# Seven block products for eight on the last two k-tiles of layer B's pairs, in a two-layer attention trunk

## The chip, the core and the metric

The kernel runs on one core of a Trainium2 chip. The metric is the time on the device in microseconds (us). Engines run side by side, each through its own list of instructions in order, and wait for each other by semaphores: TensorE (PE in the profile, its weight loads PEld), VectorE (DVE), ScalarE (ACT), GpSimd (POOL) and SyncE (SP), which issues DMA transfers. POOL issues transfers too.

## What is computed

256 positions of width 2048 go through one layer of chunked attention (A) and one of forgetting attention (B), 32 heads of 128 each, everything in float32. Cut to what matters here:

```python
# layer A
h = rms_norm(x, a_norm);  q, k, v, g = split(h @ a_w_in, 4)      # 2048 -> 4 x 4096
o = chunked_relbias_attention(q, k, v)
x = x + (o * silu(g)) @ a_w_out                                   # 4096 -> 2048
# layer B
h_kv = rms_norm(x, kv_norm);  k, v = split(h_kv @ kv_w, 2)
h = rms_norm(x, b_norm);      q, g = split(h @ b_w_in, 2)
sc = q @ k.T / sqrt(128) + decay                                  # causal, decay from a cumulative sum
o = softmax(sc) @ v
x = x + (o * silu(g)) @ b_w_out
out = rms_norm(x, final_norm)
```

## The kernel before

**Projections.** Each projection is cut into units of 512 output columns. A unit accumulates in two PSUM tiles, one for each half of 128 positions (`acc[0]`, `acc[1]`). It reads its weights in sub-blocks of two k-tiles (256 rows), 512 KB each; with 2048 rows that is eight sub-blocks a unit. To keep float32 precision, each weight block is split into a high and a low part: ACT writes `hi` (a rounded copy), DVE writes `lo` (the rest), and x is split likewise. A block product is then three matmuls of 512 columns (`hi` by x's high part, `lo` by x's high part, `hi` by x's low part). A sub-block is 2 k-tiles x 2 halves x 3 = 12 matmuls.

**Pairs.** Two heads form a group; there are 16 groups. In each layer a group needs two units: `aqk` and `avg` in layer A, `bqg` (q and gate) and `bkv` (k and v) in layer B. These two units are a pair. In layer B the weights are also multiplied by a norm's gain, a number for each row: ACT applies it in `hi` (L243), DVE in `lo` (L244), one k-tile (half a sub-block, 512 columns) at a time. In layer A there is no gain, and one instruction does a whole sub-block (L248, L249).

**Seven products.** The last sub-block of both units of a pair forms a 2 x 2 by 2 x 2 block product (two halves of positions, two k-tiles, two units). Eight block products can be had with seven, for some sums of x's blocks (`sum_up`, once for all groups) and of weight blocks. Layer A's pairs 1 to 15 do that (class `Quad`): `split` makes differences of the two raw blocks on DVE and four splits of them (`quad_hi`, `quad_lo` 0 to 3), of which three are 1024 wide and one 512; `step` issues 21 matmuls, of which four products go to PSUM tiles of their own (p1, p5, p7, p6) and three straight into the units' accumulators; ACT copies p1 out, four adds on DVE make four combinations in `comb`, and each accumulator has one of them added when it is read. Layer B's pairs take all eight sub-blocks of both units plainly.

**The feed.** `Feed` runs ahead of TensorE: six raw buffers are loaded by SP, four `hi` and four `lo` buffers hold splits. A split can be written when the matmuls of the fourth split before it are done. What stands in which order on each engine is set by the scheduler of the framework, from the order of the code and its own estimates; `tc.issue_after` pins some places.

**Attention beside it.** While a pair's matmuls run, the attention of the group before goes through the other engines, cut into steps by `yield`; `drive` calls them at the sub-blocks given by `B1_STEPS` (first unit), `B2_STEPS` (second) and `OLD_B_STEPS`. For layer B: ACT evacuates k from the accumulator of `bkv` into `qk` (L510), DVE transposes 32 x 32 blocks of q and k (`first<-qk`, L501), POOL issues 16 transfers that put the blocks in place (`sums<-first`, L504; the tile is called `sums`, since the attention uses half of that buffer), and ACT and DVE split them (`wide`, `q`). TensorE makes the scores (`s1p`, `s0p`), DVE adds the bias and finds maxima, ACT takes exponentials. DVE transposes the probabilities and the gates (`sgY`), POOL transfers them (`sgZ`), they are split (`wide<-sgZ`), TensorE makes `op`, and DVE multiplies by the gate (`oT`). On TensorE the `op` of the group before stands behind a pair's second sub-block of `bqg`, the scores of this one behind its seventh.

Of the kernel before, what the change touches and what calls it, by code (L numbers as in the profile page):

```python
# [76 lines left out]
def trunk(ctx, tc, x, x_t, gains, a_w_in, a_rel, a_w_out, kv_w, f_w, f_b, b_w_in, b_w_out, final_norm, out):  # L77
# [111 lines left out]
    class Feed:  # L189
# [31 lines left out]
        def prepare(self, ahead=True, parts=(slice(None),)):  # L221
# [12 lines left out]
            if 0 <= h < spec["kept"]:  # L234
                both = big_tile([P, 2, IL, KB, HN], F32R, f"{nm}_keep{b}")
                hi, lo = both[:, 0], both[:, 1]
            else:
                hi = stream.tile([P, IL, KB, HN], F32R, name=f"{nm}_hi{b}", tag="hi", bufs=SPLIT)
                lo = stream.tile([P, IL, KB, HN], F32R, name=f"{nm}_lo{b}", tag="lo", bufs=SPLIT)
            if spec["g0"] is not None:  # L240
                for j in range(KB):
# [1 line left out]
                    act.activation(hi[:, :, j], raw[:, :, j], AF.Copy, scale=gk)  # L243
                    dve.scalar_tensor_tensor(lo[:, :, j], raw[:, :, j], gk, r32(hi[:, :, j]),  # L244
                                             op0=OP.mult, op1=OP.subtract)
# [32 lines left out]
    class Quad:  # L278

        def __init__(self, all_, specs, b, first, last):  # L280
            self.all, self.specs, self.b, self.first, self.last = all_, specs, b, first, last

        def split(self, i):
# [3 lines left out]
            if not i:  # L287
                if not self.all.w:
                    feed.behind(t[:, :, 0, :1], -1)
                with tc.issue_after(feed.by_dve.ins) if self.all.w else nullcontext():  # L290
                    dve.tensor_sub(t[:, :, 0], two[:, :, 0], one[:, :, 0])
                    dve.tensor_sub(t[:, :, 1], two[:, :, 1], two[:, :, 0])
            src = [one, t, two[:, :, 1:], one][i]
            n = src.shape[2]
            hi = stream.tile([P, IL, KB, HN], F32R, name=f"quad_hi{i}", tag="hi", bufs=SPLIT)
            lo = stream.tile([P, IL, KB, HN], F32R, name=f"quad_lo{i}", tag="lo", bufs=SPLIT)
            feed.by_act = act.activation(hi[:, :, :n], src, AF.Copy)
            feed.by_dve = dve.tensor_sub(lo[:, :, :n], src, r32(hi[:, :, :n]))
            if not i:
                dve.tensor_sub(one[:, :, 0], two[:, :, 1], t[:, :, 0])  # L300
                dve.tensor_sub(one[:, :, 1], one[:, :, 1], one[:, :, 0])
# [738 lines left out]
```

## Time and profile before

| | us |
|---|---|
| median of three runs (1738.96 to 1740.59) | 1739.95 |
| the profiled execution | 1738.73 |
| its span | 1737.0 |
| PE busy | 1723.2 (99%) |
| DVE busy | 1377.9 (79%) |
| ACT busy | 1139.4 (66%) |
| POOL busy | 517.0 (30%) |

The profile is of one execution. A group's mean duration is from the start of an instruction to its end; since an engine begins the next one before the last has ended, the distance between two starts is shorter. In the chain of work that ended last, a row is a stretch of one engine: its start, its length, and the instructions in it. In the timeline a row has start, length, engine, line, operation, `out<-in`, shapes and count, and in brackets the idle time before it with what ended it.

### The profile page before, as it was taken

How to read it: one execution, taken by the hardware profiler on the slowest of the kernel's cores; microseconds unless marked ns; L12 is line 12 of the kernel's file. 1: busy time of each engine (PE TensorE's matmuls, PEld its weight loads, DVE VectorE, ACT ScalarE, POOL GpSimd, SP SyncE). 2: the span in 40 equal slices, each digit the busy share in tenths (PEclk: the TensorE clock that was granted, in tenths of full speed). 3: DMA queues.
4: the chain of work that ended last, by engine and by line, in shares of the span. 5: the costliest groups of instructions: out<-in, count | busy, mean ns of one | idle time of the engine just before them, and what ended most of it. 6: DMA issues, size and time to landing. Idle time of an engine off the chain costs nothing.

```text
span 1737.0 us, 25888 instructions
## 1 busy us (share of the span) xinstructions
PE 1723.2 (99%) x8303; PEld 1513.8 (87%) x8303; DVE 1377.9 (79%) x2066; ACT 1139.4 (66%) x2151; POOL 517.0 (30%) x1071
## 2 busy tenths in 40 slices
PE   9999999999999999999999999999999999999997
PEld 7888888888888888888888888888888888888886
DVE  7888888888888888989876777777777777776887
ACT  6666666666666666655567777777777777675554
POOL 1332333333333333112204333333333333333000
PEclk9999999999999999999999999999999999999999
DMA  8766767667767677677757767676777776777654
GB/s 301 245 227 227 232 230 229 232 225 230 233 226 227 227 227 227 205 252 256 241 203 235 228 226 225 226 227 226 227 227 226 227 228 227 248 229 231 224 194 145
DMA packets 143656, 396.37 MB, mean 228 GB/s; under 512 B 31104, under 2 KB 38560, under 8 KB 143392
## 3 DMA queue, kind: packets, MB, share of 16 engines
q1 hardware_dynamic: 107472, 354.25, 62.3%
q0 software_dynamic: 32256, 37.29, 6.6%
q10 hardware_dynamic: 3792, 3.17, 0.6%
q8 instruction: 66, 1.08, 0.3%
q14 instruction: 70, 0.57, 0.1%
HBM read 351.05 MB, written 4.23 MB: 205 GB/s over the span
## 4 chain that ended last, share of the span: by engine, by line
PE 97%; DVE 1%; DMA 1%; ACT 1%; SPq 0%; issue 0%; DVEq 0%; ACTq 0%
PE bkv_acc L185 19%; PE bqg_acc L185 19%; PE avg_acc L185 17%; PE aqk_acc L185 16%; PE bo_acc L185 8%; PE ao_acc L185 7%; PE p L532 1%; PE p L531 1%; PE p L530 1%; PE s0p L554 1%; PE op L594 1%; PE op L532 0%; PE s1p L532 0%; PE s1p L531 0%; PE op L531 0%; PE op L530 0%
## 5 line engine op out<-in xcount | busy, mean ns | idle before, releaser
L504 POOL DMA_DIRECT2D sums<-first x448 | 219.9, 498 | 324.8 <-DVE wide L523 147.7
L504 POOL DMA_DIRECT2D sgZ<-sgY x512 | 250.7, 497 | 173.8 <-DVE sgY L501 90.1
L244 DVE SCALAR_TENSOR_TENSOR bqg_lo<-bqg_raw,gain,bqg_hi 128x512 fp32r<-128x512 f32 x256 | 183.0, 752 | 88.1 <-ACT bqg_hi L243 88.1
L243 ACT ACTIVATE bqg_hi<-bqg_raw,gain 128x512 fp32r<-128x512 f32 x256 | 170.8, 713 | 110.0 <-PE bqg_acc L185 51.9
L244 DVE SCALAR_TENSOR_TENSOR bkv_lo<-bkv_raw,gain,bkv_hi 128x512 fp32r<-128x512 f32 x256 | 180.3, 749 | 40.8 <-ACT bkv_hi L243 39.2
L185 PE MATMUL bqg_acc<-bqg_hi,x1Th 128*128 128x512 f32 x512 | 191.4, 384 | 0.0
L185 PE MATMUL bkv_acc<-bkv_hi,x1Th 128*128 128x512 f32 x512 | 189.0, 379 | 0.0
L185 PE MATMUL bkv_acc<-bkv_hi,x1Tl 128*128 128x512 f32 x512 | 188.8, 379 | 0.0
L185 PE MATMUL bkv_acc<-bkv_lo,x1Th 128*128 128x512 f32 x512 | 188.8, 379 | 0.0
L185 PE MATMUL bqg_acc<-bqg_hi,x1Tl 128*128 128x512 f32 x512 | 188.8, 379 | 0.0
L185 PE MATMUL bqg_acc<-bqg_lo,x1Th 128*128 128x512 f32 x512 | 188.8, 379 | 0.0
L243 ACT ACTIVATE bkv_hi<-bkv_raw,gain 128x512 fp32r<-128x512 f32 x256 | 167.8, 713 | 25.8 <-PE bqg_acc L185 19.9
L185 PE MATMUL aqk_acc<-aqk_hi,xTh 128*128 128x512 f32 x452 | 167.6, 382 | 1.7 <-ACT aqk_hi L248 1.7
L185 PE MATMUL avg_acc<-avg_hi,xTh 128*128 128x512 f32 x452 | 167.4, 382 | 0.0
L185 PE MATMUL aqk_acc<-aqk_lo,xTh 128*128 128x512 f32 x452 | 166.3, 379 | 1.0 <-DVE aqk_lo L249 1.0
L185 PE MATMUL avg_acc<-avg_lo,xTh 128*128 128x512 f32 x452 | 166.1, 379 | 0.0
L185 PE MATMUL avg_acc<-avg_hi,xTl 128*128 128x512 f32 x452 | 166.1, 379 | 0.0
L185 PE MATMUL aqk_acc<-aqk_hi,xTl 128*128 128x512 f32 x452 | 166.1, 379 | 0.0
L248 ACT ACTIVATE avg_hi<-avg_raw 128x1024 fp32r<-128x1024 f32 x112 | 116.1, 1050 | 76.1 <-PE avg_acc L185 50.5
L249 DVE TENSOR_TENSOR avg_lo<-avg_raw,avg_hi 128x1024 fp32r<-128x1024 f32 x112 | 136.8, 1222 | 31.0 <-ACT avg_hi L248 31.0
L249 DVE TENSOR_TENSOR aqk_lo<-aqk_raw,aqk_hi 128x1024 fp32r<-128x1024 f32 x110 | 134.1, 1223 | 24.8 <-ACT aqk_hi L248 17.0
L248 ACT ACTIVATE aqk_hi<-aqk_raw 128x1024 fp32r<-128x1024 f32 x110 | 115.6, 1051 | 42.2 <-PE avg_acc L185 31.6
(345 smaller groups left out, 3926.2 us busy)
## 6 DMA issues: line engine op xcount, KB each, us to landing
bqg_raw<-in_b_w_in SPq DMA_DIRECT2D x128, 512.0 KB, 4.3
bkv_raw<-in_kv_w SPq DMA_DIRECT2D x128, 512.0 KB, 4.1
avg_raw<-in_a_w_in SPq DMA_DIRECT2D x127, 512.0 KB, 4.6
aqk_raw<-in_a_w_in SPq DMA_DIRECT2D x125, 512.0 KB, 4.5
ao_raw<-in_a_w_out SPq DMA_DIRECT2D x64, 512.0 KB, 4.5
bo_raw<-in_b_w_out SPq DMA_DIRECT2D x64, 512.0 KB, 4.2
sgZ<-sgY POOLq DMA_DIRECT2D x512, 40.0 KB, 3.9
sums<-first POOLq DMA_DIRECT2D x448, 32.0 KB, 3.7
```

The lines of the kernel that those rows point to most:

```text
L185: pe.matmul(acc[t], x[:, t * P:(t + 1) * P], w, start=t not in begun, stop=last and i == 2)
L243: act.activation(hi[:, :, j], raw[:, :, j], AF.Copy, scale=gk)
L244: dve.scalar_tensor_tensor(lo[:, :, j], raw[:, :, j], gk, r32(hi[:, :, j]), op0=OP.mult, op1=OP.subtract)
L248: self.by_act = act.activation(hi[:, :, j], raw[:, :, j], AF.Copy)
L249: self.by_dve = dve.tensor_sub(lo[:, :, j], raw[:, :, j], r32(hi[:, :, j]))
L504: queues[j].dma_start(out=r32(z)[j * SQ:(j + 1) * SQ, i], in_=y[i * SQ:(i + 1) * SQ, j])
L530: pe.matmul(out_, a[0], b[0], start=start, stop=False)
L531: pe.matmul(out_, a[0], b[1], start=False, stop=False)
L532: pe.matmul(out_, a[1], b[0], start=False, stop=stop)
L554: pe.matmul(s0p[:, i], q0[:, i], qkT[:, HG + i, 0], start=True, stop=True)
L594: pe.matmul(op[:, i, 1::NT], v1[:, i * DH:(i + 1) * DH], pT[:, i, NT], start=False, stop=i == HG - 1)
```

## The change

Layer B's pairs 1 to 15 get the seven products too. The last sub-blocks of `bqg` and `bkv` are left out of the plain lists; a `Quad` of both stands behind the third sub-block of `bkv` (`QUAD_STEP_B = 3`, after the seven plain ones of `bqg`). Since the weights of layer B carry gains, `split` first scales the two raw blocks in place on ACT, a k-tile at a time, four instructions in all. `comb` then holds the combinations; `add_whole` adds them onto the accumulators: `qg`'s right behind the products, where `open_b` reads them, and `kv`'s when that unit is done. The sums of x for the last two k-tiles of layer B are made once, in group 0. And the layout of all weight blocks changes: a sub-block was `[2 halves, 2 k-tiles, 256]` a partition, with a k-tile's two halves (columns that alternate in the matmul's reading) 2 KB apart, and is now `[2 k-tiles, 2 halves, 256]`, with the halves 1 KB apart and a k-tile in one run of 2 KB. The host packs the weights in that order.

```diff
+QUAD_STEP_B = 3
 def cols(v, j):
-    return v[:, :, j].rearrange("p a n -> p n a")
+    return v[:, j].rearrange("p a n -> p n a")
 ...
         def buffer(self, name):
-            ... stream.tile([P, IL, KB, HN], F32, name=name, tag="raw", bufs=RAW)
+            ... stream.tile([P, KB, IL, HN], F32, name=name, tag="raw", bufs=RAW)
 ...
     class Quad:
         def __init__(self, all_, specs, b, first, last):
+            self.w = specs[0]["g0"] is not None or all_.w
 ...
         def split(self, i):
             if not i:
-                if not self.all.w:
-                    feed.behind(t[:, :, 0, :1], -1)
+                if not self.w:
+                    feed.behind(t[:, 0, :, :1], -1)
+                if self.specs[0]["g0"] is not None:
+                    with tc.issue_after(feed.by_act.ins):
+                        for raw, sp_ in zip(self.raw, self.specs):
+                            for j in range(KB):
+                                gk = gain[:, sp_["g0"] + self.b * KB + j:][:, :1]
+                                act.activation(raw[:, j], raw[:, j], AF.Copy, scale=gk)
-                with tc.issue_after(feed.by_dve.ins) if self.all.w else nullcontext():
+                with tc.issue_after(feed.by_dve.ins) if self.w else nullcontext():
 ...
+    def paired(specs, n):
+        quad = Quad(a_quads, specs, KD // KB - 1, True, True)
+        plain = whole(specs[0]) + whole(specs[1])
+        todo.extend(plain[:n] + [(None, quad)] + plain[n:])
+        return quad
+    a_pairs = [paired(qkvg[2 * g:2 * g + 2], QUAD_STEP) for g in range(1, NG)]
 ...
-        qkvg.append(spec(f"bqg{g}", b_w_in[g], KD, g0=GB))
-        qkvg.append(spec(f"bkv{g}", kv_w[g], KD, g0=GKV))
+        qkvg.append(spec(f"bqg{g}", b_w_in[g], KD, g0=GB, quads=g > 0))
+        qkvg.append(spec(f"bkv{g}", kv_w[g], KD, g0=GKV, quads=g > 0))
 ...
+    b_pairs = [paired(qkvg[2 * g:2 * g + 2], KD // KB - 1 + QUAD_STEP_B) for g in range(NG + 1, 2 * NG)]
 ...
+    def add_whole(acc, i):
+        out = [a_quads.comb[:, i * NT + t] for t in range(NT)]
+        for t in range(NT):
+            dve.tensor_add(out[t], acc[t], out[t])
+        return out
 ...
-    def open_b(accs):
-        qk, qg = rows(UN, "qk"), accs["qg"]
+    def open_b(accs, g):
+        qk, qg = rows(UN, "qk"), add_whole(accs["qg"], 0) if g else accs["qg"]
 ...
-        accs["qg"] = drive(unit(x1T), prev if g else last[0], B1_STEPS if g else {2: 99}, {}, old, OLD_B_STEPS)
-        accs["kv"] = drive(unit(x1T), prev if g else fg, B2_STEPS if g else FORGET_STEPS, {2: lambda: open_b(accs)})
+        if g:
+            first, second = (Unit(x1T, next(order)) for _ in range(2))
+            accs["qg"] = drive(rest(first), prev, B1_STEPS, {}, old, OLD_B_STEPS)
+            def products():
+                b_pairs[g - 1].step(x1T, first, second)
+                open_b(accs, g)
+            kv = drive(rest(second), prev, B2_STEPS, {QUAD_STEP_B - 1: products})
+            accs["kv"] = add_whole(kv, 1)
+        else:
+            accs["qg"] = drive(unit(x1T), last[0], {2: 99})
+            accs["kv"] = drive(unit(x1T), fg, FORGET_STEPS, {2: lambda: open_b(accs, g)})
+            a_quads.sum_up(x1T, KD // KB - 1, sums[:, 0], a_quads.comb)
 ...
-        out.append(cols.reshape(k // KB, KB, P, HN, IL).transpose(0, 2, 4, 1, 3))
+        out.append(cols.reshape(k // KB, KB, P, HN, IL).transpose(0, 2, 1, 4, 3))
```

How this moves instructions, at three places of group 7 (the other groups are alike). In the names, the number behind `hi`, `lo` and `raw` is the sub-block, and the last number is the buffer's.

ScalarE behind the landing of the transposed q and k in `sums`, first before (L522 and L546 split q and k, L243 the sub-blocks of kv, L570 takes exponentials), then after:

```order
L522 ACTIVATE wide_11922<-sums_104 128x2x128
L522 ACTIVATE q1_11924<-sums_104 128x128
L522 ACTIVATE wide_11922<-sums_104 128x2x128
L522 ACTIVATE q1_11924<-sums_104 128x128
L546 ACTIVATE q0_11934<-sums_104 128x256
L243 ACTIVATE bkv7_hi0_11902<-bkv7_raw0_11728,gain_83 128x2x256 x2
L243 ACTIVATE bkv7_hi1_11937<-bkv7_raw1_11782,gain_83 128x2x256 x2
L243 ACTIVATE bkv7_hi2_11979<-bkv7_raw2_11808,gain_83 128x2x256 x2
L570 ACTIVATE sg_11967,sm_11969<-sg_11967,nm_11968 128x256 x2
```

```order
L535 ACTIVATE wide_12063<-sums_104 128x2x128
L535 ACTIVATE q1_12065<-sums_104 128x128
L535 ACTIVATE wide_12063<-sums_104 128x2x128
L244 ACTIVATE bkv7_hi1_12043<-bkv7_raw1_11865,gain_83 128x512 x2
L535 ACTIVATE q1_12065<-sums_104 128x128
L559 ACTIVATE q0_12075<-sums_104 128x256
L244 ACTIVATE bkv7_hi2_12078<-bkv7_raw2_11923,gain_83 128x512 x2
L297 ACTIVATE bqg7_raw7_11949<-bqg7_raw7_11949,gain_83 128x512 x2
L297 ACTIVATE bkv7_raw7_11951<-bkv7_raw7_11951,gain_83 128x512 x2
L305 ACTIVATE quad_hi0_12126<-bqg7_raw7_11949 128x1024
```

kv's first sub-block has moved ahead of the landing, and four scalings of the raw blocks and the first product's `hi` stand behind its third.

VectorE from the third sub-block of kv on (`sg<-s1p` adds the bias to the scores, L568 or L581 finds the maxima, `csc` is the softmax's factor), first before, then after:

```order
L244 SCALAR_TENSOR_TENSOR bkv7_lo2_11980<-bkv7_raw2_11808,gain_83,bkv7_hi2_11979 128x2x256
L564 SCALAR_TENSOR_TENSOR sg_11967<-s1p_11957,cb_11742 128x256 x2
L567 SCALAR_TENSOR_TENSOR sg_11967<-s0p_11958,d0_11763 128x2x128
L568 TENSOR_REDUCE nm_11968<-sg_11967 128x2 x2
L244 SCALAR_TENSOR_TENSOR bkv7_lo2_11980<-bkv7_raw2_11808,gain_83,bkv7_hi2_11979 128x2x256
L576 RECIPROCAL csc_12041<-sm_11969 128x4
L577 TENSOR_TENSOR csc_12041<-csc_12041,half_b_8598 128x4
L244 SCALAR_TENSOR_TENSOR bkv7_lo3_12002<-bkv7_raw3_11842,gain_83,bkv7_hi3_12001 128x2x256 x2
L244 SCALAR_TENSOR_TENSOR bkv7_lo4_12022<-bkv7_raw4_11862,gain_83,bkv7_hi4_12021 128x2x256 x2
L501 STREAM_TRANSPOSE sgY_12048<-sg_11967 128x1280
```

```order
L299 TENSOR_TENSOR first1_102<-bkv7_raw7_11951,bqg7_raw7_11949 128x512
L577 SCALAR_TENSOR_TENSOR sg_12108<-s1p_12098,cb_11881 128x256 x2
L580 SCALAR_TENSOR_TENSOR sg_12108<-s0p_12099,d0_11902 128x2x128
L581 TENSOR_REDUCE nm_12109<-sg_12108 128x2 x2
L300 TENSOR_TENSOR first1_102<-bkv7_raw7_11951 128x512
L306 TENSOR_TENSOR quad_lo0_12127<-bqg7_raw7_11949,quad_hi0_12126 128x1024
L589 RECIPROCAL csc_12160<-sm_12110 128x4
L308 TENSOR_TENSOR bqg7_raw7_11949<-bkv7_raw7_11951,first1_102 128x512
L590 TENSOR_TENSOR csc_12160<-csc_12160,half_b_8598 128x4
L309 TENSOR_TENSOR bqg7_raw7_11949<-bqg7_raw7_11949 128x512
L306 TENSOR_TENSOR quad_lo1_12145<-first1_102,quad_hi1_12144 128x1024
L514 STREAM_TRANSPOSE sgY_12167<-sg_12108 128x1280
```

The first difference of raw blocks, which needs three of ACT's scalings, now stands ahead of the scores, and the products' differences and splits between the scores and the gate transpose.

VectorE from the end of kv to the transpose of q and k (`first<-qk`), first before, then after; L735 is `add_whole`:

```order
L244 SCALAR_TENSOR_TENSOR bkv7_lo7_12116<-bkv7_raw7_11943,gain_83,bkv7_hi7_12115 128x2x256 x2
L244 SCALAR_TENSOR_TENSOR bqg8_lo0_12136<-bqg8_raw0_11985,gain_83,bqg8_hi0_12135 128x2x256 x2
L244 SCALAR_TENSOR_TENSOR bqg8_lo1_12156<-bqg8_raw1_12007,gain_83,bqg8_hi1_12155 128x2x256 x2
L244 SCALAR_TENSOR_TENSOR bqg8_lo2_12176<-bqg8_raw2_12027,gain_83,bqg8_hi2_12175 128x2x256 x2
L501 STREAM_TRANSPOSE first1_102<-qk_12087 128x1024
```

```order
L352 TENSOR_TENSOR comb_103<-comb_103,p5_12205 128x512
L245 SCALAR_TENSOR_TENSOR bkv7_lo6_12275<-bkv7_raw6_12084,gain_83,bkv7_hi6_12274 128x512
L735 TENSOR_TENSOR comb_103<-bqg7_acc1_11914,comb_103 128x512
L639 SCALAR_TENSOR_TENSOR gs_12269<-gs_12269,comb_103 128x256
L245 SCALAR_TENSOR_TENSOR bqg8_lo0_12295<-bqg8_raw0_12190,gain_83,bqg8_hi0_12294 128x512 x2
L639 SCALAR_TENSOR_TENSOR gs_12269<-gs_12269,comb_103 128x256
L245 SCALAR_TENSOR_TENSOR bqg8_lo1_12315<-bqg8_raw1_12212,gain_83,bqg8_hi1_12314 128x512 x2
L245 SCALAR_TENSOR_TENSOR bqg8_lo2_12335<-bqg8_raw2_12226,gain_83,bqg8_hi2_12334 128x512 x2
L735 TENSOR_TENSOR comb_103<-bkv7_acc0_11915,comb_103 128x512
L735 TENSOR_TENSOR comb_103<-bkv7_acc1_11916,comb_103 128x512
L245 SCALAR_TENSOR_TENSOR bqg8_lo3_12393<-bqg8_raw3_12240,gain_83,bqg8_hi3_12392 128x512 x2
L514 STREAM_TRANSPOSE first1_102<-qk_12264 128x1024
```

The combinations, the gate's products and two adds onto kv have come in front of the transpose, with one sub-block more of the next unit.

More of the change, by code (lines that the diff above doesn't have):

```diff
@@ L198, in buffer @@
         def buffer(self, name):
-            return self.early.pop(0) if self.early else stream.tile([P, IL, KB, HN], F32, name=name, tag="raw",
+            return self.early.pop(0) if self.early else stream.tile([P, KB, IL, HN], F32, name=name, tag="raw",
                                                                     bufs=RAW)
@@ L206, in load @@
                     first(j)
-                sp.dma_start(out=raw[:, :, j], in_=spec["w"][b][:, :, j])
+                sp.dma_start(out=raw[:, j], in_=spec["w"][b][:, j])
             return raw
@@ L263, in behind @@
         def behind(self, dst, n):
-            act.activation(dst, r32(self.ready[n][0][:, :, 0, :1]), AF.Copy)
+            act.activation(dst, r32(self.ready[n][0][:, 0, :, :1]), AF.Copy)
         def fill(self):
@@ L287, in split @@
             if not i:
-                if not self.all.w:
-                    feed.behind(t[:, :, 0, :1], -1)
-                with tc.issue_after(feed.by_dve.ins) if self.all.w else nullcontext():
[L291 to L298, printed above, removed]
+                if not self.w:
[7 more added lines that the diff above has]
+                with tc.issue_after(feed.by_dve.ins) if self.w else nullcontext():
+                    dve.tensor_sub(t[:, 0], two[:, 0], one[:, 0])
+                    dve.tensor_sub(t[:, 1], two[:, 1], two[:, 0])
+            src = [one, t, two[:, 1:], one][i]
+            n = src.shape[1]
+            hi = stream.tile([P, KB, IL, HN], F32R, name=f"quad_hi{i}", tag="hi", bufs=SPLIT)
+            lo = stream.tile([P, KB, IL, HN], F32R, name=f"quad_lo{i}", tag="lo", bufs=SPLIT)
+            feed.by_act = act.activation(hi[:, :n], src, AF.Copy)
+            feed.by_dve = dve.tensor_sub(lo[:, :n], src, r32(hi[:, :n]))
             if not i:
-                dve.tensor_sub(one[:, :, 0], two[:, :, 1], t[:, :, 0])
-                dve.tensor_sub(one[:, :, 1], one[:, :, 1], one[:, :, 0])
+                dve.tensor_sub(one[:, 0], two[:, 1], t[:, 0])
+                dve.tensor_sub(one[:, 1], one[:, 1], one[:, 0])
             return hi, lo
@@ L627, in gate_from @@
         return gs
-    first = [big_tile([P, 2, IL, KB, HN], F32, name=f"first{i}") for i in range(2)]
+    first = [big_tile([P, 2, KB, IL, HN], F32, name=f"first{i}") for i in range(2)]
     feed.early += [first[i][:, j] for i in range(2) for j in range(2)]
```

30 lines of the change are left out of this document (11 added, 19 removed).

## The prediction

> **What bounds the kernel now.** I read the head of the page, then the chain that ended last in order of time, then each engine's busy time by stage, and then the timeline of VectorE (DVE), ScalarE (ACT) and GpSimd (POOL) around one pair of layer B.
>
> ```profile
> span 1737.0 us, 25888 instructions
> PE 1723.2 (99%) x8303; PEld 1513.8 (87%) x8303; DVE 1377.9 (79%) x2066; ACT 1139.4 (66%) x2151; POOL 517.0 (30%) x1071
> ...
> 352.39 2.59 PE aqk_acc L185 x12
> 395.42 2.59 PE aqk_acc L185 x12
> 1037.14 5.18 PE bqg_acc L185 x24
> 1057.51 2.59 PE bqg_acc L185 x12
> 1060.10 20.72 PE bkv_acc L185 x96
> 1080.82 5.18 PE bqg_acc L185 x24
> 1561.22 5.18 PE bo_acc L185 x24
> ```
>
> TensorE is the bound. Twelve matmuls take 2.59 us, 215.9 ns each. A pair of layer B lasts 1080.82 - 1037.14 = 43.68 us; a pair of layer A, which already has seven products, 395.42 - 352.39 = 43.03. The difference, 0.65, is three matmuls (3 x 0.2159 = 0.648): no pair stalls in either layer. The profiled execution took 1738.73 us, 1.73 over its span; the median of the three runs shown is 1739.95, 1.2 above it. I make the sum against 1738.73 and add the 1.2 at the end.
>
> ```profile
> 355.30:398.30 43.00, 43.00 (x212) 37.93 (x211) 36.95 (x52) 27.98 (x51) 13.89 (x29) 1.00 0.70 229
> 1043.40:1087.10 43.70, 43.70 (x214) 38.55 (x213) 31.65 (x54) 31.33 (x69) 16.05 (x34) 1.00 0.71 226
> ```
>
> By stretch (length, then PE, PEld, DVE, ACT, POOL busy): DVE works 36.95 us of an A pair and 31.65 of a B pair. So 12 us of slack is what the change can draw on.
>
> **The part that is sure.** Each of the 15 changed pairs loses three of 192 matmuls: 15 x 0.648 = 9.7 us off TensorE. If nothing else ends last, that is 1729.0, or 1730.2 on the runs' median.
>
> **What DVE and ACT get for it.** These rows give start-to-start prices (an operation begins some 0.08 us before its predecessor's end).
>
> ```profile
> 362.40 1.51 DVE L501 STREAM_TRANSPOSE sgY<-sg 128x1280 f32<-128x1280 f32 x1
> 363.83 0.65 DVE L300 TENSOR_TENSOR aqk_raw<-avg_raw,first 128x512 f32<-128x512 f32 x1
> 364.40 1.22 DVE L298 TENSOR_TENSOR quad_lo<-first,quad_hi 128x1024 fp32r<-128x1024 f32 x1
> 365.53 0.69 DVE L301 TENSOR_TENSOR aqk_raw<-aqk_raw 128x512 f32<-128x512 f32 x1
> 366.13 0.69 DVE L298 TENSOR_TENSOR quad_lo<-avg_raw,quad_hi 128x512 fp32r<-128x512 f32 x1
> ...
> 1057.85 0.75 DVE L564 SCALAR_TENSOR_TENSOR sg<-s1p,cb 128x256 f32<-128x256 f32 x2
> 1058.52 0.42 DVE L567 SCALAR_TENSOR_TENSOR sg<-s0p,d 128x256 f32<-128x256 f32 x1
> 1058.85 1.01 DVE L568 TENSOR_REDUCE nm<-sg 128x2 f32<-128x512 f32 x2
> 1059.77 0.75 DVE L244 SCALAR_TENSOR_TENSOR bkv_lo<-bkv_raw,gain,bkv_hi 128x512 fp32r<-128x512 f32 x1
> 1061.46 0.18 DVE L576 RECIPROCAL csc<-sm 128x4 f32<-128x4 f32 x1 [0.95 <-ACT sg L570]
> 1062.07 2.74 DVE L244 SCALAR_TENSOR_TENSOR bkv_lo<-bkv_raw,gain,bkv_hi 128x512 fp32r<-128x512 f32 x4 [0.24 <-ACT bkv_hi L243]
> ```
>
> From the A rows: the gate transpose 1.43, a 512-wide add 0.60, a 1024-wide split 1.14. From the B rows: scores 0.33 each, both maxima 0.92, a plain sub-block's two 512-wide splits 1.33 ((2.74 - 0.75) / 3 is 0.663 for one).
>
> Per pair DVE loses four splits (2.65) and gains four differences of raw blocks, three 1024-wide splits and a 512-wide one, four combinations and four adds onto the accumulators: 2.40 + 3.42 + 0.60 + 2.40 + 2.40 = 11.2. Net +8.6: 40.2 us of a pair that should last 43.03. ACT trades four scaled halves for four scalings in place and gains three 1024-wide copies, a 512-wide one and p1's copy, about 4 us: 35 of 43. Both still fit in sum. What decides is order, since each engine runs its list in order.
>
> **The ring.** In the order after, four lists close into a ring from one pair to the next, with no TensorE step in it: the transposed q and k land in `sums`; ACT splits them, then the second and third sub-blocks of kv, then scales the two raw blocks; DVE takes its differences, and only behind those the scores; 28 us of DVE work later comes the transpose of the next q and k; POOL's sixteen transfers carry it into `sums`. I walk it from the landing.
>
> ```profile
> 1050.94 0.42 ACT L522 ACTIVATE wide<-sums 128x256 fp32r<-128x256 f32 x1 [0.66 <-DMA sums<-first]
> 1051.27 0.29 ACT L522 ACTIVATE q<-sums 128x128 fp32r<-128x128 f32 x1
> 1051.46 0.40 ACT L522 ACTIVATE wide<-sums 128x256 fp32r<-128x256 f32 x1
> 1051.77 0.29 ACT L522 ACTIVATE q<-sums 128x128 fp32r<-128x128 f32 x1
> 1051.97 0.40 ACT L546 ACTIVATE q<-sums 128x256 f32<-128x256 f32 x1
> 1052.28 1.32 ACT L243 ACTIVATE bkv_hi<-bkv_raw,gain 128x512 fp32r<-128x512 f32 x2
> 1061.33 2.55 ACT L243 ACTIVATE bkv_hi<-bkv_raw,gain 128x512 fp32r<-128x512 f32 x4
> 1063.79 1.26 ACT L581 ACTIVATE sg<-gs,csc 128x128 f32<-128x128 f32 x4
> ...
> 1081.36 1.25 DVE L501 STREAM_TRANSPOSE first<-qk 128x1024 f32<-128x1024 f32 x1 [0.93 <-ACT qk L510]
> 1083.15 3.45 POOL L504 DMA_DIRECT2D sums<-first  x7 [7.42 <-PE bqg_acc L185]
> 1088.12 4.42 POOL L504 DMA_DIRECT2D sums<-first  x9 [1.52 <-issue]
> ```
>
> ACT: wide, q, wide 0.83, the second sub-block 1.23 (four halves take 2.46), q 0.20, q0 0.31, the third sub-block 1.23, then three of the four scalings, 2 x 0.615 and the third to its end, 0.71 (1.32 - 0.615): with the hand-over **5.8**. The scaling has no row before; the nearest is the same-sized scaled copy at L243, and I take that.
>
> DVE, in its list's order: difference 0.60, scores 0.67 + 0.33, maxima 0.92, difference 0.60, first product split 1.14, reciprocal 0.21, difference 0.60, multiply 0.15, difference 0.60, second split 1.14, gate transpose 1.43, third 0.60, a wait of 0.2 for ACT, fourth 1.14 (10.3 so far); three plain sub-blocks 3.99; four combinations 2.40 with the fourth sub-block 1.33 among them; two adds onto qg 1.20 and two gate products 0.67; three sub-blocks of the next unit 3.99; only then the two adds onto kv 1.20, another sub-block 1.33, and the transpose 1.25. **27.7**. ACT's share is ready in time by the same prices (the fourth product split excepted), so DVE idles nowhere else in it.
>
> POOL: from the transpose's end (1081.36 + 1.25 = 1082.61) to ACT's read in the next pair (1050.94 + 43.68 = 1094.62), **12.0**.
>
> The ring takes 5.8 + 27.7 + 12.0 = 45.5 us, against TensorE's 43.03 and the 43.68 of now. Before, the ring is slack: the transpose stands directly behind kv's evacuation, 0.54 us after kv's last slot (1081.36 against 1080.82). So I forecast that TensorE loses three matmuls a pair and waits 2.5 us: at the fourth product's low part, at `op` (whose split stands behind the late transpose on DVE) and a little at the scores.
>
> ```profile
> 908.01 1.22 DVE L501 STREAM_TRANSPOSE first<-qk 128x1024 f32<-128x1024 f32 x1
> 922.28 0.42 ACT L522 ACTIVATE wide<-sums 128x256 fp32r<-128x256 f32 x1 [3.02 <-DMA sums<-first]
> ```
>
> Group 1's landing, at 922.28, is the first of fifteen and unchanged. Layer B's last pair then ends 14 rings later and 27.6 us behind its landing (DVE's fourth split ends at 5.8 + 10.3 = 16.1; the product's last five matmuls and four sub-blocks are 11.5): 922.28 + 14 x 45.5 + 27.6 = 1586.9, where `bo` now begins at 1561.22. That is +25.7. The output projection inherits one late `op`: its two sub-blocks before `op` end 5.2 us on, 32.8 behind the landing, while DVE is done at 33.5 + 0.7, +1.5. Sum: 1738.7 + 25.7 + 1.5 = 1765.9, 1767 on the runs' median; I say **1766**.
>
> **The remaining edits.** Halves 1 KB apart: layer A's and B's matmuls read them 2 KB apart; the nearest other distances are `zp` (512 B) and `s1p` (2 KB), both 256 columns.
>
> ```profile
> 884.10 0.27 PE L846 MATMUL zp<-x1Th,fwp 128*64 128x256 f32 x1
> 884.21 0.27 PE L847 MATMUL zp<-x1Tl,fwp 128*64 128x256 f32 x1
> ...
> 354.82 0.27 PE L530 MATMUL s1p<-wide,q 128*128 128x256 f32 x1
> 354.93 0.28 PE L531 MATMUL s1p<-wide,q 128*128 128x256 f32 x1
> ```
>
> Both start 0.11 us apart: the distance shows nothing, and I take 0. The same rows read as a rate (0.11 for half of 0.2159) bound it at 0 to 2 ns a matmul, at most 16 us over some 7,600; nothing suggests a gain. On DVE and ACT the halves merge into one run of 512; contiguous and split 512-wide adds cost alike above (L300, L301), so 0. The order of layer A's lists is unchanged. The sums of x (once, group 0: six adds and subtractions, at most 0.60 each) lie beside TensorE. SP's loads keep their number; a raw pair is held until the fourth split, as in layer A.
>
> **Rivals.** (1) *Cover holds, faster*: DVE's 40.2 us stay hidden, 1730. For it: the sum fits in 43.03, and A's pairs run without a stall at 36.95. Against it: the ring must be 2.5 us shorter than its rows; A has its `op`, scores and products in another order, so its slack proves nothing here. Decides if the ring is under 43.0. (2) *Break-even*: a ring of 43.5 to 43.9 gives 1738 to 1744. (3) *POOL's part grows*: group 1 took 922.28 - 909.23 = 13.05 for the same step; with 13.0 the ring is 46.5 and the end 14 later, 1781. The Trainium skill, "SBUF — State Buffer", section "SBUF: two separate sides", says that POOL cannot write its transfers' descriptors while a DVE operation holds the port pair they share; with a busier DVE that speaks for this one. By that rule the 1781 would be the forecast; the trace has 13.05 once and 12.0 in the steady pairs, so I leave it a rival.
>
> **Chances.** Ring near 45.5 (44.2 to 46.0): 0.64, with its own range 1749 to 1773 (14 us for each 1 us). Ring longer: 0.15. Break-even: 0.06. Cover holds: 0.15. A measurement tells 0.2% (3.5 us) from no change: faster 0.15, same 0.06, slower 0.79. The range 1738 to 1782 leaves out cover and the tail above.
>
> **What would show it.** Right: 45 to 46 us between the starts of neighbouring B pairs; TensorE waiting for DVE at the fourth product and at `op`; ACT's `wide<-sums` behind the DMA; the qk transpose some 6 us behind kv's last matmul, not 0.5; DVE busy 40 us a pair. Wrong: pairs of 43.0 and no waits on TensorE (then a DVE price above is too high), matmuls off 215.9 ns (then the layout), or waits on raw loads.

## The result, and the profile after

| kernel | median of the runs, us | ratio to before | 95% interval |
|---|---|---|---|
| before (same chip) | 1739.67 (1738.96 to 1740.59) | | |
| after | 1781.99 (1780.85 to 1782.98) | 1.0243 | 1.0225 to 1.0260 |

The change makes the kernel 42.3 us slower. The forecast was slower, 1766, with 1738 to 1782: the direction and the mechanism hold, and the size is 16 us short. That the median still lies inside the range, by 0.01 us, is luck: two of the four runs (1782.64 and 1782.98) lie above it.

First the head of the page after, and the shares of the chain that ended last.

```profile
span 1779.1 us, 26149 instructions
...
PE 1738.7 (98%) x8258; PEld 1508.9 (85%) x8258; DVE 1493.1 (84%) x2252; ACT 1197.0 (67%) x2227; POOL 516.5 (29%) x1071
...
PE 72%; DVE 12%; ACT 10%; issue 4%; DMA 2%; POOL 0%; DVEq 0%; SPq 0%; ACTq 0%
```

Then the waits of TensorE's weight loads (who waited, for whom: us in total, times, longest).

```profile
PEld bqg_acc L544 <- DVE quad_lo L306: 15.0, 14, 1.1
PEld op L544 <- DVE wide L536: 11.9, 14, 1.0
PEld s1p L543 <- ACT q L535: 6.1, 10, 1.1
PEld s1p L545 <- DVE q L536: 5.6, 12, 0.5
PEld bkv_acc L544 <- DVE quad_lo L306: 3.9, 14, 1.1
```

The 45 matmuls fewer are there (8303 to 8258), but 28% of the chain now lies outside TensorE's work, and TensorE waits 10 to 14 times at each of the places that the prediction named: the fourth product's low part, `op`, the scores. PE's busy time rose although it does less, so part of what it loses is counted as busy: over fourteen pairs the starts of its matmuls lie some 49 us further apart than their spacing in stretches without a wait (0.216 us for 512 columns, 0.108 for 256), about 13 of them at the fourth product, 13 at `op`, 16 at the scores. The waits tell where, the busy share does not.

Where the time stands, by the chain in order of time: layer B begins 0.4 us later than before (860.3 against 859.9), `bo` begins 41.4 us later.

```profile
1602.59 5.18 PE bo_acc L186 x24
1609.24 12.95 PE bo_acc L186 x60
1623.71 28.49 PE bo_acc L186 x132
```

Before, these stood at 1561.22, 1567.52 and 1581.59. The stretch of 132 matmuls takes 28.49 us in both: a matmul costs what it did. From `bo`'s start to the end of the span are 176.5 us (175.8 before).

Now one ring, walked as in the prediction, in the timeline of ACT, DVE and POOL. Its start is the read: ACT's first split (`wide<-sums`) of the landed blocks.

```profile
1110.47 0.42 ACT L535 ACTIVATE wide<-sums 128x256 fp32r<-128x256 f32 x1 [4.59 <-DMA sums<-first]
1114.26 1.32 ACT L297 ACTIVATE bqg_raw<-bqg_raw,gain 128x512 f32<-128x512 f32 x2
1115.48 1.32 ACT L297 ACTIVATE bkv_raw<-bkv_raw,gain 128x512 f32<-128x512 f32 x2
1116.22 0.69 DVE L299 TENSOR_TENSOR first<-bkv_raw,bqg_raw 128x512 f32<-128x512 f32 x1 [1.04 <-ACT bkv_raw L297]
...
1140.33 1.28 DVE L735 TENSOR_TENSOR comb<-bkv_acc,comb 128x512 f32<-128x512 f32 x2
1141.52 1.40 DVE L245 SCALAR_TENSOR_TENSOR bqg_lo<-bqg_raw,gain,bqg_hi 128x512 fp32r<-128x512 f32 x2
1142.85 1.24 DVE L514 STREAM_TRANSPOSE first<-qk 128x1024 f32<-128x1024 f32 x1
1144.62 5.39 POOL L517 DMA_DIRECT2D sums<-first  x11 [8.81 <-DVE wide L536]
1150.30 2.08 POOL L517 DMA_DIRECT2D sums<-first  x4 [0.28 <-DMA sums<-first]
1152.58 0.50 POOL L517 DMA_DIRECT2D sums<-first  x1 [0.20 <-issue]
1155.94 0.42 ACT L535 ACTIVATE wide<-sums 128x256 fp32r<-128x256 f32 x1 [3.22 <-DMA sums<-first]
```

From the read at 1110.47 to the first difference 5.75 us; from there to the end of the transpose (1144.09) 27.87; from there to the next read 11.85. The sum is the ring, 45.47. At its turn each engine waits for the one before in the ring (in the brackets), and TensorE is not among them. POOL's bracket names the split `wide` that DVE begins right at the end of the transpose; what POOL sends is `first`, the transpose's result, and its first issue stands 0.54 us behind the transpose's end in all fourteen rings, as in the kernel before.

The first and the last of fourteen such rings:

```profile
924.20 0.42 ACT L535 ACTIVATE wide<-sums 128x256 fp32r<-128x256 f32 x1 [3.76 <-DMA sums<-first]
...
1574.34 0.42 ACT L535 ACTIVATE wide<-sums 128x256 fp32r<-128x256 f32 x1 [4.08 <-DMA sums<-first]
```

(1574.34 - 924.20) / 14 = 46.44 us. Taken apart by the same three rows in every ring:

| link, mean of 14 | forecast | after |
|---|---|---|
| ACT, landing to first difference | 5.8 | 5.75 (5.75 in all) |
| DVE, to the end of the transpose | 27.7 | 27.90 (27.76 to 28.33) |
| POOL and landing, to the read | 12.0 | 12.79 (11.85 to 14.27) |
| ring | 45.5 | 46.44 (45.47 to 48.05) |

### The profile page after: what moved, and what is told of

It is laid out like the page before. It is cut to its first block, busy times and chain, and to the rows that moved or that the text cites. A ratio compares the mean times of both kernels' runs of the same rounds, so it can differ in the third digit from the quotient of the medians.

```text
span 1779.1 us, 26149 instructions
## 1 busy us (share of the span) xinstructions
PE 1738.7 (98%) x8258; PEld 1508.9 (85%) x8258; DVE 1493.1 (84%) x2252; ACT 1197.0 (67%) x2227; POOL 516.5 (29%) x1071
## 4 chain that ended last, share of the span: by engine, by line
PE 72%; DVE 12%; ACT 10%; issue 4%; DMA 2%; POOL 0%; DVEq 0%; SPq 0%; ACTq 0%
PE avg_acc L186 16%; PE aqk_acc L186 16%; PE bqg_acc L186 11%; PE bo_acc L186 7%; PE ao_acc L186 7%; PE bkv_acc L186 4%; DVE bqg_lo L245 3%; DVE bkv_lo L245 3%; ACT bkv_hi L244 2%; ACT quad_hi L305 2%; DVE comb L735 2%; PE p L544 1%; PE p L543 1%; PE p L545 1%; ACT sg L583 1%
## 5 line engine op out<-in xcount | busy, mean ns | idle before, releaser
L245 DVE SCALAR_TENSOR_TENSOR bkv_lo<-bkv_raw,gain,bkv_hi 128x512 fp32r<-128x512 f32 x226 | 158.4, 748 | 21.9 <-ACT bkv_hi L244 20.2
L186 PE MATMUL bkv_acc<-bkv_hi,x1Th 128*128 128x512 f32 x452 | 168.1, 383 | 0.0
L186 PE MATMUL bqg_acc<-bqg_hi,x1Th 128*128 128x512 f32 x452 | 167.4, 382 | 0.0
L244 ACT ACTIVATE bqg_hi<-bqg_raw,gain 128x512 fp32r<-128x512 f32 x226 | 149.2, 712 | 26.4 <-PE bqg_acc L186 8.8
L186 PE MATMUL bkv_acc<-bkv_hi,x1Tl 128*128 128x512 f32 x452 | 166.6, 380 | 0.0
L186 PE MATMUL bkv_acc<-bkv_lo,x1Th 128*128 128x512 f32 x452 | 166.5, 380 | 0.0
L186 PE MATMUL bqg_acc<-bqg_lo,x1Th 128*128 128x512 f32 x452 | 166.1, 379 | 0.0
L186 PE MATMUL bqg_acc<-bqg_hi,x1Tl 128*128 128x512 f32 x452 | 166.1, 379 | 0.0
L245 DVE SCALAR_TENSOR_TENSOR bqg_lo<-bqg_raw,gain,bqg_hi 128x512 fp32r<-128x512 f32 x226 | 158.7, 748 | 8.6 <-ACT bqg_hi L244 8.6
L244 ACT ACTIVATE bkv_hi<-bkv_raw,gain 128x512 fp32r<-128x512 f32 x226 | 144.8, 710 | 19.8 <-PE bqg_acc L186 17.5
```

The lines of the kernel that those rows point to most:

```text
L186: pe.matmul(acc[t], x[:, t * P:(t + 1) * P], w, start=t not in begun, stop=last and i == 2)
L244: self.by_act = act.activation(hi[:, j], raw[:, j], AF.Copy, scale=gk)
L245: self.by_dve = dve.scalar_tensor_tensor(lo[:, j], raw[:, j], gk, r32(hi[:, j]), op0=OP.mult, op1=OP.subtract)
```

## The experiments

Every ratio is against the kernel before, run on the same chip. The rows come from several chips, on which the kernel before took 1739.05 to 1739.82, so times of different rows can be compared to about 1 us.

| run | us | ratio to before, 95% interval |
|---|---|---|
| layout_alone | 1738.39 | 0.9994 (0.9986 to 1.0003) |
| products_alone | 1779.15 | 1.0234 (1.0220 to 1.0248) |
| act_issues_quarter | 1753.23 | 1.0080 (1.0067 to 1.0094) |
| act_issues_half | 1751.20 | 1.0070 (1.0056 to 1.0083) |
| double_in_ring | 1795.03 | 1.0320 (1.0306 to 1.0335) |
| double_off_ring | 1776.75 | 1.0212 (1.0196 to 1.0228) |
| first_unit | 1771.88 | 1.0181 (1.0167 to 1.0195) |
| first_unit_op_later | 1746.64 | 1.0041 (1.0028 to 1.0053) |
| scale_ahead | 1745.82 | 1.0036 (1.0023 to 1.0050) |
| ahead_and_quarter | 1739.79 | 0.9999 (0.9990 to 1.0008) |
| ahead_quarter_k | 1739.56 | 0.9998 (0.9989 to 1.0007) |
| all_op_later | 1737.10 | 0.9989 (0.9980 to 0.9998) |

**Which half of the change costs?**

```diff
 # layout_alone: the new layout, layer B's pairs as before (the list of loads and the loop over groups too)
-qkvg.append(spec(f"bqg{g}", b_w_in[g], KD, g0=GB, quads=g > 0))     # bkv likewise
+qkvg.append(spec(f"bqg{g}", b_w_in[g], KD, g0=GB))
 # products_alone: the seven products, blocks laid out as before
-return v[:, j].rearrange("p a n -> p n a")                          # and all tiles and slices likewise
+return v[:, :, j].rearrange("p a n -> p n a")
```

> The kernel before, with nothing of the change but the new layout of the weight blocks (a k-tile's two halves 1 KB apart instead of 2 KB); all pairs of layer B take their eight sub-blocks plainly. Ring theory (the whole rise comes from the list DVE - POOL - ACT that closes from pair to pair in layer B): the layout costs nothing, 1739.7 us within 3, twelve matmuls 2.59 us, a B pair 43.7. Rival, the layout slows TensorE's reads or the splits: some of the 42 us stand here already, 1743 to 1756.

> The changed kernel with the weight blocks in their old layout; the seven products stay where the change puts them. Ring theory: 1782 within 4, rings of 46.4 us. Rival, the layout: what the layout costs is missing, 1768 to 1778.

The layout alone is worth -2.4 to +0.5 us; the products alone cost 39.9, and the interval of their ratio overlaps that of the whole change (1.0225 to 1.0260). The rings of products_alone are 46.2 us. The rise comes from the products; no cost of the layout can be seen.

**Is it the ring, or the volume of work on DVE?** Two kernels with more to do on DVE, at two places of its list.

```diff
 # double_in_ring: in Quad.split, layer B
 feed.by_dve = dve.tensor_sub(lo[:, :n], src, r32(hi[:, :n]))
+if i in (1, 3) and self.specs[0]["g0"] is not None:
+    feed.by_dve = dve.tensor_sub(lo[:, :n], src, r32(hi[:, :n]))
 # double_off_ring: in Feed.prepare
 self.by_dve = dve.scalar_tensor_tensor(lo[:, j], raw[:, j], gk, r32(hi[:, j]), ...)
+if b in (5, 6) and nm[:3] == "bqg": self.by_dve = dve.scalar_tensor_tensor(...)   # the same again
```

> The changed kernel, with two of the four product splits on DVE (the second and the fourth, 1.14 us each) written twice, which changes no result. They stand between the landing and the next qk transpose. The scheduler answers by moving kv's second sub-block, 1.23 us of ACT, from behind the landing to ahead of it. Ring theory: + 2.28 - 1.23 = + 1.05 us a ring, 14 rings: 1782 + 15 = 1797, range 1791 to 1803. Rival, volume: 2.28 us more DVE a pair, wherever it stands, + 34 (1816), the same as for the next kernel (2.65 us, + 40) in proportion.

> The changed kernel, with the splits of bqg's sixth and seventh sub-blocks on DVE (four of 0.663 us, 2.65 a pair) written twice, which changes no result. They stand behind the qk transpose and ahead of the landing, where DVE waits for POOL's transfers anyway. Ring theory: nothing, 1782, range 1779 to 1786, though DVE has more to do than in the kernel with the doubled product splits. Rival, volume: + 15 x 2.65 = + 40, 1822.

2.28 us more in the ring cost 13.0 over the change (15 forecast, since 1.23 of ACT's work left the ring; its ACT link is 4.61 in the mean, its ring 47.39). 2.65 us more beside the ring cost nothing: 1776.75 is below the change's 1781.99, and 2 us below the forecast range. Volume would have made both slower by 34 to 40. This is the sharpest evidence: the same engine, splits in both, and the place in its list decides.

The second kernel also bears on the reason given for rival 3. First the POOL link of the change that is walked above, as a stretch (length, then PE, PEld, DVE, ACT, POOL busy, clock, DMA share, GB/s), then one of the kernel with the doubled splits beside the ring:

```profile
1144.09:1155.94 11.85, 11.50 (x57) 10.14 (x58) 7.77 (x14) 5.71 (x12) 7.86 (x16) 1.00 0.84 259
```

```profile
1142.10:1154.33 12.23, 11.87 (x59) 10.46 (x60) 10.26 (x18) 5.72 (x12) 7.84 (x16) 1.00 0.73 232
```

DVE is busy 10.26 us of it instead of 7.77, and POOL's sixteen issues take 7.84 instead of 7.86; the link's mean over 14 rings is 12.35, against 12.79. DVE's work does not slow POOL's issues here: over 14 rings the sixteen issues take 7.96 us in the mean in either kernel. The Trainium skill, "SBUF — State Buffer", section "SBUF: two separate sides", names as what holds the shared port pair a DVE operation in a two-port mode, or one with two SBUF inputs while GpSimd reads SBUF; my rival had left these conditions out. The splits doubled here have two SBUF inputs and POOL issued beside them at its usual pace: that contradicts the shorter form that I gave the rule, not the rule as it is written; no run here was made to test a two-port mode.

**Shorten POOL's link.** ACT issues a part of the transfers.

```diff
-rest_of = attention(g, biases, qk, lambda: (v, gs), halfB, oB, line=(1, 2), home=home)
+rest_of = attention(g, biases, qk, lambda: (v, gs), halfB, oB, (pool, pool, pool, act), (1, 2), home)
 # act_issues_half: (pool, act, pool, act)
```

> The changed kernel, but in layer B ACT issues four of the sixteen transfers that carry the transposed q and k (as in layer A) and POOL twelve. Ring theory: POOL's link shortens by four issues of 0.5 us, 2.0, and ACT spends its 2.4 us of issuing on no link; the ring goes from 46.4 to 44.4 and the time from 1782 to 1754 (14 x 2.0 less); range 1750 to 1762. Rival, volume on DVE and ACT: no gain, 1780 to 1786, since ACT gets more to do. Rival, waits for raw weights or for cb from SP: no gain, 1782.

The time is 1753.23, 0.8 from the forecast: the ring is 44.58, its POOL link 10.82. ACT's and DVE's links stay at 5.76 and 28.00, so the gain is the link's. The issues in that kernel, on ACT and POOL:

```profile
1134.42 2.44 ACTq L517 DMA_DIRECT2D sums<-first  x4
1134.93 5.39 POOL L517 DMA_DIRECT2D sums<-first  x11 [8.98 <-DVE wide L536]
```

> The changed kernel, but in layer B ACT issues eight of the sixteen transfers of the transposed q and k, POOL the other eight. Ring theory: with four on ACT the measured rings were 44.6 us and the link from the transpose to the read 10.9. With eight, POOL is done at 0.5 + 8 x 0.5 = 4.5 us and ACT at about 0.5 + 8 x 0.61 = 5.4, both with some 4 us to land: a link of 9.5, a ring of 43.2, just over TensorE's 43.03, and the time 1753 - 14 x 1.4 = 1734, range 1730 to 1741. Rival, ACT's volume: its 4.9 us of issuing stand in front of the next splits of bqg, so that TensorE waits there, and the time stays at 1750 or rises.

A miss, 1751.20, 10 above the range: the link only falls to 10.67, not to 9.5. In the timeline of ACT and DVE in that kernel:

```profile
1088.98 6.01 ACTq L517 DMA_DIRECT2D sums<-first  x8
1095.04 0.63 ACT L616 ACTIVATE oBh<-oT 128x512 fp32r<-128x512 f32 x1 [6.15 <-DMA sums<-first]
1095.70 0.69 DVE L617 TENSOR_TENSOR oBl<-oT,oBh 128x512 fp32r<-128x512 f32 x1 [4.12 <-ACT oBh L616]
```

Eight issues hold ACT for 6.01 us, 0.75 each, where four took 2.44, 0.61 each. What is queued behind them on ACT, `oBh`, six splits of weights and two copies of v, then comes before its read of the landed blocks. That read waits for the landing in none of the fourteen rings, so the ring closes through ACT's list instead of POOL's.

**Move the products.** Behind the fifth sub-block of `bqg`, as in layer A, and then `op` later too.

```diff
-b_pairs = [paired(qkvg[2 * g:2 * g + 2], KD // KB - 1 + QUAD_STEP_B) ...]
+b_pairs = [paired(qkvg[2 * g:2 * g + 2], 5) ...]
-            accs["qg"] = drive(rest(first), prev, B1_STEPS, {}, old, OLD_B_STEPS)
+            products = {4: lambda: b_pairs[g - 1].step(x1T, first, second)}
+            accs["qg"] = drive(rest(first), prev, B1_STEPS, products, old, OLD_B_STEPS)
 ...
+            kv = drive(rest(second), prev, B2_STEPS, {2: lambda: open_b(accs, g)})
 # first_unit_op_later, in addition
-OLD_B_STEPS = {0: 1, 1: 99}
+OLD_B_STEPS = {1: 1, 2: 99}
```

> The changed kernel with the seven products moved from behind the third sub-block of bkv to behind the fifth sub-block of bqg (as layer A has them); the same products, sums, scalings and adds, in another order. Ring theory: differences, product splits and combinations now stand on DVE while POOL's transfers are under way, ahead of the landing, and no longer between the landing and the next transpose. By the profiled rows DVE's list from the landing to the end of the next qk transpose then holds about 21 us, with 1 us of ACT ahead and 12.8 of POOL behind: a ring of 35, under TensorE's 43.03. The full 15 x 0.648 = 9.7 us come off: 1730, range 1728 to 1738. Rival, volume (DVE's 40 us and ACT's 36 us a pair are too much wherever they stand, or a busier DVE slows POOL): 1765 to 1785, pairs of 45 to 46.

A miss by 42 us. The ring through the landing is gone, as expected (the landed blocks lie there before DVE's list comes to them), but another closes at about 45.3 (the median of the pairs is 45.2). TensorE's longest wait in that kernel:

```profile
PE op L543 <- ACT wide L535: 16.3, 15, 3.3
```

And the two ends of the long link, in the timeline of TensorE and ACT:

```profile
1114.70 0.38 PE L544 MATMUL s1p<-wide,q 128*128 128x256 f32 x1 [0.17 <-DVE wide L536]
1139.39 0.72 ACT L535 ACTIVATE wide<-sgZ 128x256 fp32r<-128x256 f32 x2 [3.38 <-DMA sgZ<-sgY]
1139.86 0.38 PE L543 MATMUL op<-wide,vh 128*128 128x256 f32 x1 [0.94 <-ACT wide L535]
```

From the scores to `op` are 25.2 us of softmax, transpose, transfers and split, and from `op` to the next scores 20.1 us, nearly all of it TensorE's own list, into which the move put the 21 products (at the scores it waits about 0.2 us a pair for DVE's split). I had looked for the next cycle only where the old one was.

> The products behind the fifth sub-block of bqg, as in the run first_unit, and in addition op on TensorE one sub-block later (behind bqg's third, not its second). That run (1771.9) had pairs of 45.3 us, and TensorE waited at op for the transfers of sg, not for q and k. Theory of a second ring: scores, softmax, transpose of sg, POOL's transfers, op took 25.2 us in it (1114.70 to 1139.86), and from op to the next scores TensorE has 20.1 us of its own work (five sub-blocks and the products, which the move put between op and the scores): 45.3. One sub-block fewer between op and the scores gives 42.7, under 43.03: 1731, range 1729 to 1738. Rival, volume: no gain, 1768 to 1775, the same waits elsewhere.

One sub-block fewer between the two takes 25 us off; the ring theory had 41, so this is a miss too. TensorE now stands at the scores in all pairs (waits of its weight loads).

```profile
PEld s1p L544 <- DVE wide L536: 9.0, 15, 1.1
PEld op L543 <- ACT wide L535: 3.8, 3, 2.0
```

DVE comes to the split of q and k only behind the four combinations, and pairs without a longer transfer last 43.55 us. What closes the cycle there is not settled. One candidate is the list from the landing of `sg` through these, the scores, the softmax and `sg`'s transfers. But the chain that ended last goes another way in these pairs: from the scores through 32 us of TensorE's own matmuls to the fourth product's `quad_hi` on ACT, which waits for TensorE, and from there through DVE's splits and combinations to the next scores. No run tells the two apart.

**Leave the products where the change has them, and empty the ring.** First the scalings and the first two differences two sub-blocks earlier.

```diff
 # end of Feed.prepare
+            if len(self.loaded) > LOOK:                       # LOOK = 2
+                q, i = self.loaded[LOOK][:2]
+                if q is None and i[1] == 0: i[0].ahead()
 # class Quad: the scalings and two differences move out of split(0)
+        def ahead(self):
+            with tc.issue_after(feed.by_act.ins): ...         # four scalings of the raw blocks
+            with tc.issue_after(feed.by_dve.ins):
+                dve.tensor_sub(t[:, 0], two[:, 0], one[:, 0])
+                dve.tensor_sub(t[:, 1], two[:, 1], two[:, 0])
```

> The changed kernel, with the four scalings of the raw blocks (ACT) and the first two differences (DVE, 0.60 each) issued two sub-blocks earlier, ahead of the landing of q and k instead of behind it; nothing else moved. Ring theory: the 5.75 us from the landing to the first difference fall away as a link. DVE now goes from the landing through the splits of q and k, kv's third sub-block, the scores and the products: by the rows of the changed kernel its fourth product split ends 12.4 us behind the landing instead of 16.1 (13.2 if the load of cb, which ACT waits for ahead of the gates, comes in between), so the ring falls from 46.4 to 42.7 to 43.5, about TensorE's 43.03: 1731 to 1741, middle 1737. Rival, POOL alone is at fault (its link had 12.8 where 12.0 was forecast) or volume: 1776 to 1784.

36 us come off, 1745.82, 5 above the upper end. In the timeline of ACT and DVE, from a landing:

```profile
1101.42 0.42 ACT L550 ACTIVATE wide<-sums 128x256 fp32r<-128x256 f32 x1 [1.38 <-DMA sums<-first]
1110.85 1.51 DVE L529 STREAM_TRANSPOSE sgY<-sg 128x1280 f32<-128x1280 f32 x1 [0.23 <-ACT sg L609]
1113.56 1.23 DVE L306 TENSOR_TENSOR quad_lo<-bqg_raw,quad_hi 128x1024 fp32r<-128x1024 f32 x1 [0.45 <-ACT quad_hi L305]
```

The fourth split ends 13.4 us behind the landing, as the forecast had with cb in between (13.2). Yet the rings run from 42.80 to 46.05, mean 43.98, above the forecast's 42.7 to 43.5. I had taken 12.8 for POOL's link, and here it is 13.09 in the mean, with two long ones (14.58 and 15.26); the way from the landing to the transpose's end is 0.2 longer than forecast. The ring is still above TensorE's 43.03 in all but two pairs, so there is no slack that could take up a long link, and a short one would give back nothing below 43.03.

So I took more out of the ring than the mean asks for: ACT issues a quarter of the transfers; ACT's work on `cb`, which waits for a load, goes behind kv's sixth sub-block; then k without its detour through ACT; then `op` later.

```diff
 # ahead_and_quarter, in addition: (pool, pool, pool, act) as above, and
+                with tc.issue_after(accs["behind"].ins) if g else nullcontext():  # feed.by_act when the products are issued
                     act.activation(d0[:, i], cb[:, i, :P], AF.Identity, ...)
 # ahead_quarter_k, in addition
-            accs["kv"] = add_whole(kv, 1);  evac_scaled(kv, 0, GC, rsB, qk[:, :, GC:])
+            dve.scalar_tensor_tensor(qk[:, t, GC:], kv[t][:, :GC], rsB[:, t:t + 1], comb[:, t, :GC], op0=OP.mult, op1=OP.add)
+            dve.tensor_add(comb[:, t, GC:], kv[t][:, GC:], comb[:, t, GC:])
 # all_op_later, in addition
+OLD_B_STEPS = {1: 1, 2: 99}
```

> As scale_ahead, and in addition ACT issues four of the sixteen transfers of q and k (as in act_issues_quarter), and ACT's bias work on cb and d0 is put behind kv's sixth sub-block, so that ACT no longer waits for the load of cb ahead of the gates. Ring theory: 29.8 us to the end of the transpose and a POOL link of 10.9, ring 40.7, 2.3 us under TensorE's 43.03, enough for most of the longer links (12 to 13 in act_issues_quarter): no stall left, the full 9.7 us come off, 1730, range 1729 to 1736: faster than both kernels. Rival, something else closes a ring near 43.5 (the transfers of sg and op, as in first_unit): 1737 to 1745.

> As ahead_and_quarter, and in addition k is scaled and combined in one step on DVE (two operations of 256 columns straight into the tile that is transposed, with the combination scaled by ACT beforehand) instead of two 512-wide adds on DVE and an evacuation on ACT; v's two 256-wide adds come behind the transpose or beside it. Ring theory: the ring is under TensorE's time already, so this adds nothing to the steady state: 1730, within 2 us of ahead_and_quarter. If that one is left with waits at op (whose split stands behind the transpose on DVE), this one has fewer, by up to 1 us a pair: up to 15 us better.

Both stand where before stands, nearly 10 us above their forecasts of 1730. In ahead_quarter_k the ring through the landing is off the path: ACT's read waits for the landing in none of the 14 rings, and from read to read are 43.51 to 43.56 us in nine of them. TensorE shows two waits in layer B, but its weight loads show what is left. The two answers on waits:

```profile
PE op L559 <- DVE wide L551: 0.8, 2, 0.4
...
PEld op L559 <- DVE wide L551: 5.7, 14, 0.7
```

And TensorE's timeline at one `op`:

```profile
1390.72 0.27 PE L558 MATMUL op<-wide,vh 128*128 128x256 f32 x1
1391.05 0.38 PE L559 MATMUL op<-wide,vh 128*128 128x256 f32 x1
1391.26 0.28 PE L560 MATMUL op<-wide,vl 128*128 128x256 f32 x1
1391.37 0.28 PE L558 MATMUL op<-wide,vh 128*128 128x256 f32 x1
```

The first matmuls of `op` start 0.33 and 0.21 us apart, where these take 0.11. Over 14 pairs such gaps at `op` sum to 7.0 us (by all starts on TensorE from 926.3 to 1536.6), which is the 0.5 that a pair lasts over 43.03. The wait is for the operand `wide`, whose low part DVE makes behind the qk transpose.

> As ahead_quarter_k, and in addition op on TensorE one sub-block later (behind bqg's third). That run's pairs last 43.52 us: the seven products have taken the 0.65 us off, but no more than 0.15 is left of it against 43.67, since in all pairs TensorE stands about 0.4 us at op, whose split on DVE comes behind the qk transpose. Theory (the ring has slack, op alone is left): pairs of 43.03 to 43.1 and 1739.6 - 15 x 0.45 = 1733, range 1731 to 1736: faster than before and than the change. Rival, the later op pushes its split, oT and what follows into DVE's work ahead of the landing, and the ring or the scores become the bound again: 1738 to 1743.

1737.10, 2.0 us below before (0.3 to 3.5 by the interval, so barely clear of the noise) and 45 below the change. It is the only version whose interval lies below before, and it is 1.1 above its forecast range. Pairs are 43.42 and the gaps at `op` 5.4 in 14. Putting `op` later helped little because its split moved with it, as ACT's rows show: it stands behind a marker (`wide<-bqg_hi`) that pins it to the feed.

```profile
1390.57 0.21 ACT L271 ACTIVATE wide<-bqg_hi 128x2 fp32r<-128x2 f32 x1 [2.27 <-DVE bqg_lo L246]
1390.68 0.70 ACT L245 ACTIVATE bqg_hi<-bqg_raw,gain 128x512 fp32r<-128x512 f32 x1
1391.29 0.71 ACT L550 ACTIVATE wide<-sgZ 128x256 fp32r<-128x256 f32 x2
```

Setting that marker one sub-block earlier (`line=(1, 1)`) would be the next step; it was not tried, and the 5 us that it may bring are argued, not shown.

## Why the prediction was right, and where its size was off

- **The ring from pair to pair: right, and shown.** Its links were read off before; ACT's is off by 0.05, DVE's by 0.2. Shortening a link shortens the time by 14 times as much (act_issues_quarter: POOL's link 1.97 shorter, 14 x 1.97 = 27.6 of the 28.8 us gained); 2.65 us of work beside the ring cost nothing. The size was less good: a ring of 46.44 lies outside the 44.2 to 46.0 that had the chance of 0.64, in the branch "ring longer" with 0.15.
- **The step that failed: POOL's link of 12.0.** It is the term of the sum that was mis-sized: 12.79 measured, 14 x 0.79 = 11 of the 15 us missing. I had subtracted the end of one pair's transpose (1082.61) from the read of the pair before plus a period. The read of that very pair stood in the trace, on ACT:

```profile
1095.88 0.42 ACT L522 ACTIVATE wide<-sums 128x256 fp32r<-128x256 f32 x1 [1.93 <-DMA sums<-first]
```

  That is 13.27, not 12.0. Over all fourteen pairs of before the link has a mean of 12.32 and runs from 11.24 to 15.53: a link off the path varies unseen, and on the path its mean counts, all of it. With 12.32 the sum would have been 1766 + 4.5 = 1770.5. Where the last 0.47 a ring lies can be read off, but not why. POOL's sixteen issues take 7.96 us in both kernels, and the pauses between them 0.94 and 1.00. From the end of the last issue to ACT's read are 2.89 us before and 3.29 after, so nearly all of it is the landing of the last transfers. Links of 12.35 to 12.89 in the kernels that keep POOL's sixteen issues in the ring say that part of it may be scatter between executions.
- **The rest of the sum.** DVE's 0.2 is 2.8 us in 14 rings. Group 1's landing, taken as unchanged at 922.28, stands at 924.20 (+1.9). The tail behind the last landing is 28.25, not 27.6 (+0.65), and `bo` inherits 0.7, not 1.5 (-0.8). 13.2 + 1.9 + 0.65 - 0.8 = 14.9, the difference from the forecast span of 1764.2 to 1779.1.
- **Rival 3, POOL's part grows:** its number, 1781, came out, and its reason did not. Of the 0.79 over the 12.0, 0.32 was there before the change, and the rest isn't in POOL's issuing. Nor is DVE busier during the link: 7.8 us of it after, 9.0 before.
- **Rival 1, cover holds:** out. Its sum (40 us of DVE fit in 43) was right, since DVE is busy 39.2 us in a ring of 45.5, but the sum does not decide.
- **Layout at nothing:** right; the 0 to 16 us that its bound left open are excluded. (The bound itself was half of what its rows give: 0.22 for two times 256 columns against 0.2159 is 4 ns a matmul of 512, so 31 us; that is excluded too.)
- **What was to be seen:** the three waits on TensorE, matmuls at 2.59 for twelve and DVE busy about 40 us a pair (39.2) are as told. Pairs are 46.4, just over the 45 to 46. The transpose starts 4.5 us behind kv's last matmul (1138.37 to 1142.85 in the ring above), not 6.

## What to carry to other kernels

An engine with slack in sum can still set the pace when its list closes a cycle with other lists: follow the lists from one period to the next until the chain comes back, add up the links, and compare the sum with the bound engine's period, for every cycle, not for the first one found. Price a link by its mean over all periods, from rows of the same period, and leave as much slack as it varies. Look for the place in the list where that engine waits anyway: here 2.65 us of work cost nothing there, and moving the scalings and two differences out of the cycle took 36 us off.

## What the runs showed of the hardware that was not expected

- Three of POOL's long links fall on the same groups in before and after: those that end with the reads at 1095.88, 1314.83 and 1491.20 (links of 13.27, 13.85, 15.53) and at 1110.47, 1341.39 and 1527.86 (13.23, 14.08, 14.27). In the first two POOL stands for 1.5 and 1.7 us between two issues with nothing in the profile that it waits for ("issue" in brackets), in both kernels. What it does there is open. The first of them after, in POOL's timeline (before, it is the row at 1088.12 in the prediction):

```profile
1102.74 4.39 POOL L517 DMA_DIRECT2D sums<-first  x9 [1.53 <-issue]
```

- An issue costs ACT 0.61 us in a run of four, 0.75 in a run of eight, and POOL 0.49, and for that time ACT does nothing else.
